# The last quarter of W_down as a plain product, and normed rows in the buffers of W_down's raw quarters

## The chip, the cores and the metric

The kernel runs on one core of one Trainium2 chip, in one launch. The metric is the device time of that launch in microseconds (us), the median over runs. A difference of about 0.2% can be told from no change.

Five engines work side by side: TensorE (PE: matmuls, with PEld for the weight loads), VectorE (DVE), ScalarE (ACT), GpSimd (POOL), and SyncE (SP), which here issues the DMAs. Each takes its instructions strictly in the order fixed when the program was built, and an instruction that waits holds up what stands behind it on its engine.

## What is computed

A two-layer encoder trunk on 512 tokens of width 1024, all in float32. The attention half of a layer is the same in both kernels; the part that matters is the end of each layer:

```python
def reference(x, ...):                       # x: (1, 512, 1024)
    for l in range(2):
        h = rms_norm(x, attn_norm_g[l])
        ...                                  # four mixers and gates give `merged`
        x = x + merged @ w_out[l]            # w_out: 1024 x 1024
        hm = rms_norm(x, mlp_norm_g[l])
        u = jnp.square(jax.nn.relu(hm @ w_up[l]))   # w_up: 1024 x 4096
        x = x + u @ w_down[l]                # w_down: 4096 x 1024
    return x
```

## The kernel before, in words

**Arithmetic.** Each float32 operand is split into a high part `hi` (a cast on ACT, L215) and a low part `lo` (a subtraction on DVE, L216) in the type TensorE reads; `split` does both. A product is three matmuls: hi by hi, hi by lo, lo by hi (`mm3`, L285 to L287, or L1232). The 512 tokens are four tiles of 128 rows (`X[0]` to `X[3]`, tokens t0 to t3), and contraction runs in blocks of 128, eight for 1024 rows.

**Weights.** `chunk` fetches W_in, W_out and W_up in units: a DMA on SP into `w_raw` (three buffers), then a split into `w_hi` and `w_lo` (four buffers each).

**The stages of a layer.** After attention, `run` reads X back (four DMAs, L1274), reads the norm's gain (`norm_g`, L321) and calls `add_rows` for W_out: three chunks of 256, 384 and 384 output columns, four units each, 8 blocks by 4 token tiles by 3 matmuls per chunk (96 matmuls). Each token's sum is added to X on DVE (L1095), and its squares are taken on ACT for the norm. `norm` computes the reciprocal root on DVE, writes normed rows `norm_h` (four buffers of 512 columns, L344), transposes them on TensorE (L222) and splits them into `h_hi` and `h_lo`.

Then come four blocks j of 1024 hidden features. `up(j)` makes the features `u` of block j in eight tiles of 128, with a yield after each. `add_product` multiplies `u` by rows 1024j to 1024j+1023 of W_down with seven products of half-size blocks p0 to p6 (24 matmuls of 512 columns each, 168 in all) in place of the eight that a plain product takes; for that it builds sums of quarters of `u` (`left_sums`: `l_sum`, `l_hi`, `l_lo`) and of W_down (`right_sums`: raw quarters by DMA into `r_raw`, six buffers of 128x1024; sums in place at L1184; `r_hi`, `r_lo`). The product of block j-1 is stepped between the feature tiles of `up(j)`, so its sums are made under matmuls of `up`. The product of the last block, j = 3, has no `up` after it: it runs alone at the end of the layer, and its sums of W_down are made on GpSimd instead of DVE (`alone`, L1219). After that X is written to `x_save` (layer 0, L1296), normed, and the next layer begins; in layer 1 the rows of the result leave by `out_y` (L1212).

**Order.** A scheduler fixes each engine's order when the program is built, from the order of the code, the buffers in each pool and its own estimate of times. An `r_raw` DMA can be put as early as a buffer of its tag is free, so which tiles share buffers has a say in which DMA stands where in SP's queue.

## Time and profile before

| | us |
|---|---|
| median of 3 runs | 1885.83 (1883.5 to 1886.43) |
| the profiled execution, its time | 1886.97 |
| its span, first to last instruction | 1885.2 |
| TensorE busy in it | 1791.2 (95%) |
| VectorE busy | 1310.0 (69%) |
| ScalarE busy | 952.3 (51%) |
| GpSimd busy | 424.5 (23%) |

The page gives shares over the whole span; stages inside it differ, so what follows is read stage by stage, from stretches of the trace. In the trace L216 is one line for every `lo`, and the tile names tell which one it is. A matmul's own duration overlaps its neighbours', so a rate is read from the starts of two matmuls and the count between them. A number in brackets behind a row is the idle time of the engine ahead of it, with what ended that time; `PEclk` is TensorE's granted clock, in tenths by slice or as a share of full speed.

### The profile page before, as it was taken

The numbers are of one execution on the slowest core, as the hardware profiler recorded it, in microseconds if no ns is written. First come the engines' busy times: TensorE is split into PE (matmuls) and PEld (weight loads), VectorE is DVE, ScalarE is ACT, GpSimd is POOL, SyncE is SP. The second block draws the span as 40 slices with busy tenths as digits, with TensorE's granted clock in tenths as the row PEclk, the third lists the DMA queues.
The fourth block names the chain that finished last, engine by engine and source line by source line (L and its number), as shares of the span: only waits on it lengthen the run. The fifth ranks groups of instructions, "written<-read, shape, count | busy, mean of one in ns | idle before, by whom it ended". The sixth has DMA issues, their size and how long they took to land.

```text
span 1885.2 us, 26257 instructions
## 1 busy us (share of the span) xinstructions
PE 1791.2 (95%) x9152; PEld 1538.3 (82%) x9152; DVE 1310.0 (69%) x2623; ACT 952.3 (51%) x1907; POOL 424.5 (23%) x1183
## 2 busy tenths in 40 slices
PE   6998999999999999999799989999999899999997
PEld 5897988787888888888588979887878798888876
DVE  6677866687656367675977878666875655675857
ACT  3565674455433444554446656645553334554543
POOL 2462353323200000000413604632412000000022
PEclk9998999999999999999899989999999999999998
DMA  4312122122244323323132221222222522323221
GB/s 161 119 52 70 57 81 76 51 68 61 88 127 167 101 71 109 115 82 128 56 113 96 75 59 51 78 70 77 64 64 86 196 76 90 116 83 126 81 73 67
DMA packets 64677, 168.70 MB, mean 89 GB/s; under 512 B 7968, under 2 KB 11552, under 8 KB 64544
## 3 DMA queue, kind: packets, MB, share of 16 engines
q1 hardware_dynamic: 64544, 167.02, 28.0%
q8 instruction: 72, 1.18, 0.3%
q14 instruction: 61, 0.50, 0.1%
HBM read 162.80 MB, written 4.19 MB: 89 GB/s over the span
## 4 chain that ended last, share of the span: by engine, by line
PE 74%; DVE 10%; POOL 6%; issue 4%; DMA 3%; ACT 2%; SPq 1%; POOLq 0%; DVEq 0%; ACTq 0%
PE mm L285 17%; PE mm L286 17%; PE mm L287 17%; PE u L1232 10%; PE mm L1232 4%; PE tp L222 4%; PE s L603 2%; DVE w_lo L216 2%; POOL rs_w_qk L235 2%; DMA w_raw<-in_wflat 1%; POOL rs_y_qk L238 1%; POOL rs_w_qk L236 1%; PE y L630 1%; POOL rs_w_qk L237 1%; PE y L629 1%
## 5 line engine op out<-in xcount | busy, mean ns | idle before, releaser
L285 PE MATMUL mm<-h_hi,w_hi 128*128 128x512 f32 (+1 forms) x1104 | 425.4, 387 | 1.8 <-DVE sig L1028 1.0
L287 PE MATMUL mm<-h_hi,w_lo 128*128 128x512 f32 (+1 forms) x1104 | 421.3, 386 | 4.7 <-DVE w_lo L216 2.4
L286 PE MATMUL mm<-h_lo,w_hi 128*128 128x512 f32 (+1 forms) x1104 | 423.8, 385 | 1.4 <-DVE h_lo L216 1.4
L216 DVE TENSOR_TENSOR w_lo<-w_raw,w_hi 128x768 fp32r<-128x768 f32 (+2 forms) x313 | 284.0, 920 | 106.6 <-ACT w_hi L215 104.8
L215 ACT CAST w_hi<-w_raw 128x768 fp32r<-128x768 f32 (+2 forms) x313 | 239.7, 774 | 178.3 <-PE mm L286 92.6
L287 PEld LDWEIGHTS mm<-h_hi,w_lo 128*128 128x128 f32 x1104 | 208.7, 189 | 45.1 <-DVE w_lo L216 3.9
L285 PEld LDWEIGHTS mm<-h_hi,w_hi 128*128 128x128 f32 x1104 | 208.7, 190 | 42.9 <-DVE sig L1028 2.9
L286 PEld LDWEIGHTS mm<-h_lo,w_hi 128*128 128x128 f32 x1104 | 209.1, 190 | 40.4 <-DVE h_lo L216 1.8
L216 DVE TENSOR_TENSOR r_lo<-r_raw,r_hi 128x1024 fp32r<-128x1024 f32 x112 | 145.3, 1298 | 127.1 <-ACT r_hi L215 126.8
L1184 POOL TENSOR_TENSOR r_raw<-r_raw 128x1024 f32<-128x1024 f32 x16 | 47.5, 2974 | 789.7 <-DVE r_lo L216 777.3
L287 PE MATMUL mm<-w_hi,h_lo 128*128 128x384 f32 (+1 forms) x576 | 189.5, 330 | 3.1 <-DVE h_lo L216 3.1
L286 PE MATMUL mm<-w_lo,h_hi 128*128 128x384 f32 (+1 forms) x576 | 189.5, 331 | 1.8 <-DVE w_lo L216 1.7
L285 PE MATMUL mm<-w_hi,h_hi 128*128 128x384 f32 (+1 forms) x576 | 188.8, 333 | 1.0 <-ACT v L529 0.5
L215 ACT CAST r_hi<-r_raw 128x1024 fp32r<-128x1024 f32 x112 | 117.6, 1050 | 110.6 <-PE u L1232 64.6
L235 POOL TENSOR_TENSOR rs_w_qk<-rs_y_qk 128x4 f32<-128x4 f32 (+2 forms) x216 | 62.0, 287 | 364.4 <-DVE rs_y_qk L233 301.4
L1232 PE MATMUL u<-r_lo,l_hi 128*128 128x512 f32 x320 | 128.5, 403 | 8.8 <-DVE r_lo L216 6.3
L1232 PE MATMUL u<-r_hi,l_lo 128*128 128x512 f32 x320 | 128.3, 402 | 5.1 <-DVE l_lo L216 5.1
L1232 PE MATMUL u<-r_hi,l_hi 128*128 128x512 f32 x320 | 123.7, 400 | 6.2 <-ACT l_hi L215 4.7
L287 PEld LDWEIGHTS mm<-w_hi,h_lo 128*128 128x128 f32 x576 | 109.9, 191 | 4.2 <-DVE h_lo L216 3.5
L286 PEld LDWEIGHTS mm<-w_lo,h_hi 128*128 128x128 f32 x576 | 109.9, 191 | 3.6 <-DVE w_lo L216 2.7
L285 PEld LDWEIGHTS mm<-w_hi,h_hi 128*128 128x128 f32 x576 | 109.7, 192 | 2.6 <-ACT v L529 0.7
L1122 ACT ACTIVATE relu<-mm 128x512 f32<-128x512 f32 x64 | 38.3, 599 | 140.0 <-PE mm L287 140.0
(184 smaller groups left out, 3539.4 us busy)
## 6 DMA issues: line engine op xcount, KB each, us to landing
w_raw<-in_wflat SPq DMA_DIRECT2D x232, 384.0 KB, 3.2
r_raw<-in_wflat SPq DMA_DIRECT2D x64, 512.0 KB, 3.5
w_raw<-in_wflat SPq DMA_DIRECT2D x80, 256.0 KB, 2.7
x<-in_x SPq DMA_DIRECT2D x8, 512.0 KB, 6.2
d_full<-in_mask_d SPq DMA_DIRECT2D x8, 448.0 KB, 4.6
x_save<-x SPq DMA_DIRECT2D x4, 512.0 KB, 2.6
x<-x_save SPq DMA_DIRECT2D x4, 512.0 KB, 5.3
out_y<-x SPq DMA_DIRECT2D x8, 256.0 KB, 2.0
```

What stands on the lines that cost most here:

```text
L215: self.nc.scalar.copy(hi, src)
L216: self.nc.vector.tensor_tensor(lo, src, hi.bitcast(F32), op=ALU.subtract)
L222: self.nc.tensor.transpose(out, in_, self.ident_r if short else self.ident)
L235: eng.tensor_tensor(w, y, y, op=ALU.mult)
L236: eng.tensor_tensor(w, w, v, op=ALU.mult)
L285: nc.tensor.matmul(ps, st[0], mv[0], start=first, stop=False)
L286: nc.tensor.matmul(ps, st[0], mv[1], start=False, stop=False)
L287: nc.tensor.matmul(ps, st[1], mv[0], start=False, stop=last)
L603: self.nc.tensor.matmul(ps, q[:, qc], k[:, kc], start=i == 0, stop=i == len(ks) - 1)
L1122: nc.scalar.activation(r, ps, AF.Relu)
L1184: eng.tensor_tensor(a, a, b, op=ALU.add)
L1232: nc.tensor.matmul(ps[q], a[:, k, toks], b, start=first and i == 0, stop=end and i == 2, skip_group_check=True)
```

## The change

The last block (rows 3072 to 4095 of W_down) is no longer an `add_product`. Its `u` is split in four quarters (`left_split`, into a new tag "left" of eight buffers that all left operands share), and `add_rows` multiplies it plainly in chunks of 256, 384 and 384 columns, with W_down's rows through `w_raw`, `w_hi` and `w_lo`: 96 matmuls of 256 columns and 192 of 384, where 168 of 512 stood. The sums on GpSimd and the last block's `l_sum` and `r_*` tiles are gone. While `up(3)` runs, block 2's product is stepped one feature tile later (`j < 3 or i`), so its p6 stands behind `up`'s last feature tile. And `norm` writes its rows as tiles of two halves that, in the two norms inside the MLP part, take buffers of the tag "r_raw".

```diff
@@ -75,7 +75,7 @@
 EVAC = 'act'
 NLO, NHI, NRAW = 4, 4, 3
 
-NLEFT, NRIGHT, NSPLIT = 3, 6, 2
+NLEFT, NRIGHT, NSPLIT = 8, 6, 2
 BACKLOG = 1.0
 STREAM = "D0 gD1 D1 A0 A1 gD2 zD2 gD0 zD0 zD1 B0 B1 B2 gA0 zA0 gA2 C0 zA2 gA1 zA1 C1 gB1 zB1 gC1 gB2 gB0 zB0 zB2 gC0 zC1 zC0 gC2 zC2"
 
@@ -321,7 +321,7 @@
         self.nc.sync.dma_start(g, gain.partition_broadcast(P))
         return g
 
-    def norm(self, pool, X, ms, g):
+    def norm(self, pool, X, ms, g, tag="norm_h", bufs=2):
 
         nc = self.nc
         hi = self.hp.tile([P, KD, S], F32R, name="h_hi", tag="h_hi")
@@ -338,9 +338,10 @@
             for _ in range(3):
                 stt(w, y, y, vh, op0=ALU.mult, op1=ALU.mult)
                 stt(y, w, 1.5, y, op0=ALU.add, op1=ALU.mult)
+            both = pool.tile([P, 2, S], F32, name=tag, tag=tag, bufs=bufs)
             for half in range(2):
                 cs = slice(half * S, half * S + S)
-                h = pool.tile([P, S], F32, name="norm_h", tag="norm_h", bufs=4)
+                h = both[:, half, :]
                 stt(h, X[t][:, cs], y, g[:, cs], op0=ALU.mult, op1=ALU.mult)
                 ps = self.sps.tile([P, 4, P], F32, name="tp", tag="s")
                 for j in range(4):
@@ -1082,15 +1083,15 @@
         return hi, lo
 
 
-    def add_rows(self, pool, X, act, layer, name, k0, ms=None, order=None, out=None):
+    def add_rows(self, pool, X, act, layer, name, k0, ms=None, order=None, out=None, chunks=((0, 256), (256, 384), (640, 384))):
 
         nc = self.nc
-        chunks = list(self.col_chunks(0, D)) if ms is None else [(0, 256), (256, 384), (640, 384)]
         for i, (c0, w) in enumerate(chunks):
             units = self.chunk(layer, name, k0, KD, [(c0, w)], order)
             for t in range(NT):
                 ps = self.mm.tile([P, S], F32, name="mm", tag="mm")
-                self.tm_group(ps[:, 0:w], act, slice(t * P, (t + 1) * P), units)
+                for k, (row, hi, lo) in enumerate(units):
+                    self.mm3(ps[:, 0:w], act(row, t), (hi, lo), k == 0, k == KD - 1)
                 x = X[t][:, c0:c0 + w]
                 nc.vector.tensor_tensor(x, x, ps[:, 0:w], op=ALU.add)
                 if out is not None:
@@ -1130,19 +1131,20 @@
 
 
 
+    def left_split(self, pool, src):
+        hi, lo = (pool.tile([P, KD // 2, S // 2], F32R, name=x, tag="left", bufs=NLEFT) for x in ("l_hi", "l_lo"))
+        self.split(hi, lo, src)
+        return hi, lo
+
     def left_sums(self, pool, x, eng):
 
         h, kh = S // 2, KD // 2
         x11, x12, x21, x22 = x[:, 0:kh, 0:h], x[:, kh:, 0:h], x[:, 0:kh, h:], x[:, kh:, h:]
 
-        def put(src):
-            hi = pool.tile([P, kh, h], F32R, name="l_hi", tag="l_hi", bufs=NLEFT)
-            lo = pool.tile([P, kh, h], F32R, name="l_lo", tag="l_lo", bufs=NLEFT)
-            self.split(hi, lo, src)
-            return hi, lo
+        put = lambda src: self.left_split(pool, src)
 
         def total(a, b, op):
-            s = pool.tile([P, kh, h], F32, name="l_sum", tag="l_sum", bufs=2)
+            s = pool.tile([P, kh, h], F32, name="l_sum", tag="left", bufs=NLEFT)
             eng.tensor_tensor(s, a, b, op=op)
             return s
 
@@ -1199,25 +1201,17 @@
         add(w11, w21)
         yield put(w11)
 
-    def add_product(self, pool, X, x, layer, name, k0, alone, ms=None, out=None):
+    def add_product(self, pool, X, x, layer, name, k0):
 
         nc = self.nc
         n = D // 2
         bank = {}
 
-        def onto(t, nh, ps, op, last=False):
+        def onto(t, nh, ps, op):
             x = X[t][:, nh * n:nh * n + n]
             nc.vector.tensor_tensor(x, x, ps, op=op)
-            if last and out is not None:
-                nc.sync.dma_start(out[t * P:(t + 1) * P, nh * n:nh * n + n], x)
-            if last and ms is not None:
-                part = pool.tile([P, 1], F32, name=f"ms{len(ms[t])}", tag=f"ms{len(ms[t])}", bufs=4)
-                self.squares(pool, x, part)
-                ms[t].append(part)
-
-
-        eng = nc.gpsimd if alone else nc.vector
-        left, right = self.left_sums(pool, x, nc.vector), self.right_sums(pool, layer, name, k0, eng)
+
+        left, right = self.left_sums(pool, x, nc.vector), self.right_sums(pool, layer, name, k0, nc.vector)
         for p, ((hi, lo), w) in enumerate(zip(left, right)):
 
             if p in (0, 1):
@@ -1240,14 +1234,14 @@
                 elif p == 2:
                     onto(q, 1, ps[q], ALU.subtract)
                 elif p == 3:
-                    onto(q, 1, ps[q], ALU.add, True)
+                    onto(q, 1, ps[q], ALU.add)
                 elif p == 4:
                     onto(2 + q, 0, ps[q], ALU.add)
-                    onto(2 + q, 1, ps[q], ALU.subtract, True)
+                    onto(2 + q, 1, ps[q], ALU.subtract)
                 elif p == 5:
-                    onto(q, 0, ps[q], ALU.add, True)
+                    onto(q, 0, ps[q], ALU.add)
                 else:
-                    onto(2 + q, 0, ps[q], ALU.add, True)
+                    onto(2 + q, 0, ps[q], ALU.add)
             yield
 
     def run(self):
@@ -1274,27 +1268,34 @@
                     nc.sync.dma_start(X[t], x_dram[t])
                 g = self.load_gain(pool, I["mlp_norm_g"][layer])
                 ms = [[] for _ in range(NT)]
-                self.add_rows(pool, X, act, layer, "out", 0, ms, self.merges)
-                self.hT = self.norm(pool, X, ms, g)
+                mine = lambda k, t: tuple(x[:, k, t * P:(t + 1) * P] for x in act)
+                self.add_rows(pool, X, mine, layer, "out", 0, ms, self.merges)
+                self.hT = self.norm(pool, X, ms, g, "r_raw", NRIGHT)
                 if not last:
                     g = self.load_gain(pool, I["attn_norm_g"][layer + 1])
                 prev = None
                 for j in range(4):
                     u = pool.tile([P, KD, S], F32, name="u", tag="u", bufs=2)
-                    for _ in self.up(pool, layer, j, u):
-                        if prev is not None:
+                    for i, _ in enumerate(self.up(pool, layer, j, u)):
+
+                        if prev is not None and (j < 3 or i):
                             next(prev, None)
-                    end = j == 3
-                    ms = [[] for _ in range(NT)] if end and not last else None
-                    prev = self.add_product(pool, X, u, layer, "down", j * KD, end, ms, self.out if end and last else None)
-                for _ in prev:
-                    pass
+                    if j < 3:
+                        prev = self.add_product(pool, X, u, layer, "down", j * KD)
+
+                parts = {}
+                for kh in range(2):
+                    for th in range(2):
+                        parts[kh, th] = self.left_split(pool, u[:, 4 * kh:4 * kh + 4, th * (S // 2):(th + 1) * (S // 2)])
+                act = lambda k, t: tuple(x[:, k % 4, t % 2 * P:t % 2 * P + P] for x in parts[k // 4, t // 2])
+                ms = [[] for _ in range(NT)] if not last else None
+                self.add_rows(pool, X, act, layer, "down", 3 * KD, ms, None, self.out if last else None)
                 if not last:
                     xs = self.dram.tile([S, D], F32, name=f"x_save{layer}")
                     x_dram = [xs[t * P:(t + 1) * P, :] for t in range(NT)]
                     for t in range(NT):
                         nc.sync.dma_start(x_dram[t], X[t])
-                    self.hT = self.norm(pool, X, ms, g)
+                    self.hT = self.norm(pool, X, ms, g, "r_raw", NRIGHT)
 
 
 
```

Three places in the engines' orders show what moves. The first is SP's queue from the reads of X at the start of layer 0's MLP part. First the kernel before (`r_raw` here are quarters of W_down for block 0, the first eight `w_raw` the last two chunks of W_out, and the four after them W_up's):

```order
L1274 DMA x_6478<-in_x 128x1024
L1274 DMA x_6479<-in_x 128x1024
L1274 DMA x_6480<-in_x 128x1024
L321 DMA norm_g<-in_mlp_norm_g 128x1024
L1169 DMA r_raw<-in_wflat 128x1024 x6
L248 DMA w_raw<-in_wflat 128x768 x12
L321 DMA norm_g<-in_attn_norm_g 128x1024
```

The changed kernel:

```order
L1268 DMA x_6474<-in_x 128x1024
L1268 DMA x_6475<-in_x 128x1024
L1268 DMA x_6476<-in_x 128x1024
L321 DMA norm_g<-in_mlp_norm_g 128x1024
L248 DMA w_raw<-in_wflat 128x768 x12
L1171 DMA r_raw<-in_wflat 128x1024 x4
L321 DMA norm_g<-in_attn_norm_g 128x1024
L1171 DMA r_raw<-in_wflat 128x1024 x2
```

Twelve `w_raw` now stand ahead of the first `r_raw`, and the six `r_raw` are in two parts around the next norm's gain. Layer 1 shows the same move.

The second place is SP's queue at the end of layer 0. Before, from the last quarters of block 2's W_down to the writes of X:

```order
L1169 DMA r_raw<-in_wflat 128x1024
L248 DMA w_raw<-in_wflat 128x768
L1169 DMA r_raw<-in_wflat 128x1024
L248 DMA w_raw<-in_wflat 128x768 x4
L1169 DMA r_raw<-in_wflat 128x1024 x2
L1296 DMA x_save_9559<-x_6477 128x1024
L1296 DMA x_save_9559<-x_6478 128x1024
L1296 DMA x_save_9559<-x_6479 128x1024
L1296 DMA x_save_9559<-x_6480 128x1024
```

Changed, from block 2's last quarters. Of the five `w_raw` of 128x512 the last four, and of the eleven of 128x768 the first eight, are W_down's last 1024 rows; the seven others of 128x768 are the next layer's first weights:

```order
L1171 DMA r_raw<-in_wflat 128x1024 x2
L248 DMA w_raw<-in_wflat 128x512 x5
L248 DMA w_raw<-in_wflat 128x768 x11
L1297 DMA x_save_9655<-x_6473 128x1024
L1297 DMA x_save_9655<-x_6474 128x1024
L1297 DMA x_save_9655<-x_6475 128x1024
L248 DMA w_raw<-in_wflat 128x768 x3
L1297 DMA x_save_9655<-x_6476 128x1024
L248 DMA w_raw<-in_wflat 128x768
```

The last block's weights now come as `w_raw`; two parts of the next layer's weights stand behind writes of X.

The third is DVE's order at the norm of tokens t2 and t3 between W_out and `up(0)`, layer 0. Before:

```order
L344 SCALAR_TENSOR_TENSOR norm_h<-x_6479,norm_y,norm_g 128x512 x2
L340 SCALAR_TENSOR_TENSOR norm_y<-norm_w,norm_y 128x1
L339 SCALAR_TENSOR_TENSOR norm_w<-norm_y,norm_vh 128x1
L340 SCALAR_TENSOR_TENSOR norm_y<-norm_w,norm_y 128x1
L344 SCALAR_TENSOR_TENSOR norm_h<-x_6480,norm_y,norm_g 128x512 x2
L216 TENSOR_TENSOR h_lo<-tp,h_hi 128x4x128 x4
L216 TENSOR_TENSOR w_lo<-w_raw,w_hi 128x768 x4
L216 TENSOR_TENSOR l_lo<-u,l_hi 128x1024
L216 TENSOR_TENSOR w_lo<-w_raw,w_hi 128x512 x4
L216 TENSOR_TENSOR w_lo<-w_raw,w_hi 128x768 x4
L1146 TENSOR_TENSOR l_sum<-u 128x1024
```

Changed:

```order
L345 SCALAR_TENSOR_TENSOR r_raw<-x_6475,norm_y,norm_g 128x512 x2
L340 SCALAR_TENSOR_TENSOR norm_y<-norm_w,norm_y 128x1
L339 SCALAR_TENSOR_TENSOR norm_w<-norm_y,norm_vh 128x1
L340 SCALAR_TENSOR_TENSOR norm_y<-norm_w,norm_y 128x1
L345 SCALAR_TENSOR_TENSOR r_raw<-x_6476,norm_y,norm_g 128x512 x2
L216 TENSOR_TENSOR h_lo<-tp,h_hi 128x4x128 x2
L216 TENSOR_TENSOR r_lo<-r_raw,r_hi 128x1024
L216 TENSOR_TENSOR h_lo<-tp,h_hi 128x4x128
L216 TENSOR_TENSOR r_lo<-r_raw,r_hi 128x1024
L1186 TENSOR_TENSOR r_raw<-r_raw 128x1024
L216 TENSOR_TENSOR h_lo<-tp,h_hi 128x4x128
L1186 TENSOR_TENSOR r_raw<-r_raw 128x1024
```

Between the `h_lo` of t2 and t3 there now stand the first `r_lo` and a sum of raw quarters of block 0, which before were done during W_out's product.

## Rows read from the trace of the kernel before

**Rows 1.** The page: TensorE's busy time, its clock in 40 slices, one group.
```profile
PE 1791.2 (95%) x9152; PEld 1538.3 (82%) x9152; DVE 1310.0 (69%) x2623; ACT 952.3 (51%) x1907; POOL 424.5 (23%) x1183
...
PEclk9998999999999999999899989999999999999998
```

**Rows 2.** Windows: us; PE, PEld, DVE, ACT, POOL busy (count); PEclk; DMA share; GB/s.
```profile
563.84:603.70 39.86, 36.23 (x194) 35.72 (x193) 25.21 (x53) 14.37 (x30) 0.00 (x0) 0.91 0.47 171
700.00:800.00 100.00, 100.00 (x441) 82.63 (x440) 66.32 (x73) 48.79 (x61) 0.00 (x0) 1.00 0.34 110
899.14:955.11 55.97, 44.43 (x169) 33.50 (x168) 50.86 (x64) 24.25 (x33) 18.75 (x7) 0.88 0.20 66
1492.98:1533.30 40.32, 35.27 (x194) 34.55 (x193) 25.24 (x53) 14.46 (x30) 0.00 (x0) 0.96 0.49 173
1828.76:1881.28 52.52, 44.00 (x169) 33.71 (x167) 42.88 (x37) 19.63 (x20) 17.87 (x7) 0.90 0.14 50
577.00:582.90 5.90, 5.90 (x18) 5.73 (x19) 2.21 (x4) 1.23 (x4) 0.00 (x0) 0.51 0.25 68
```

**Rows 3.** TensorE's timeline, last product of layer 0, two of six waits: start, duration.
```profile
909.46 1.22 PE L1232 MATMUL u<-r_hi,l_hi 128*128 128x512 f32 x2 [4.70 <-ACT l_hi L215]
...
940.20 0.51 PE L1232 MATMUL u<-r_lo,l_hi 128*128 128x512 f32 x1 [2.32 <-DVE norm_v L333]
```

**Rows 4.** DVE and GpSimd there, and a `w_lo` at W_out's end.
```profile
897.04 10.16 DVE L216 TENSOR_TENSOR w_lo<-w_raw,w_hi 128x768 fp32r<-128x768 f32 x4
...
893.62 11.89 POOL L1184 TENSOR_TENSOR r_raw<-r_raw 128x1024 f32<-128x1024 f32 x4 [374.73 <-DVE r_lo L216]
...
602.90 0.96 DVE L216 TENSOR_TENSOR w_lo<-w_raw,w_hi 128x768 fp32r<-128x768 f32 x1
```

**Rows 5.** TensorE's timeline: plain matmuls at full clock, 384 and 256 columns.
```profile
571.13 0.34 PE L285 MATMUL mm<-w_hi,m_hi 128*128 128x384 f32 x1
...
573.04 0.34 PE L287 MATMUL mm<-w_hi,m_lo 128*128 128x384 f32 x1
...
959.00 0.28 PE L286 MATMUL mm<-w_lo,h_hi 128*128 128x256 f32 x1
...
960.91 0.28 PE L287 MATMUL mm<-w_hi,h_lo 128*128 128x256 f32 x1
```

**Rows 6.** W_out's product, layer 0: SP, DVE, ACT and TensorE in turn.
```profile
559.12 5.18 SPq L1169 DMA_DIRECT2D r_raw<-in_wflat  x6
565.31 43.82 SPq L248 DMA_DIRECT2D w_raw<-in_wflat  x12
...
562.76 0.96 DVE L216 TENSOR_TENSOR w_lo<-w_raw,w_hi 128x768 fp32r<-128x768 f32 x1 [0.67 <-ACT w_hi L215]
...
576.12 0.83 ACT L215 CAST w_hi<-w_raw 128x768 fp32r<-128x768 f32 x1 [5.89 <-DMA w_raw<-in_wflat]
...
577.00 1.33 PE L285 MATMUL mm<-w_hi,m_hi 128*128 128x384 f32 x3 [3.62 <-ACT w_hi L215]
```

**Rows 7.** ACT's timeline, W_out's product of layer 1.
```profile
1506.68 0.83 ACT L215 CAST w_hi<-w_raw 128x768 fp32r<-128x768 f32 x1 [6.63 <-DMA w_raw<-in_wflat]
```

**Rows 8.** DVE's last `h_lo` of layer 0's MLP norm; SP's next issues of W_up.
```profile
616.70 1.37 DVE L216 TENSOR_TENSOR h_lo<-tp,h_hi 128x512 fp32r<-128x512 f32 x2 [0.81 <-ACT h_hi L215]
...
625.80 14.53 SPq L248 DMA_DIRECT2D w_raw<-in_wflat  x5
```

**Rows 9.** The page's groups of splits, and its DMA issues with landing times.
```profile
L215 ACT CAST r_hi<-r_raw 128x1024 fp32r<-128x1024 f32 x112 | 117.6, 1050 | 110.6 <-PE u L1232 64.6
...
w_raw<-in_wflat SPq DMA_DIRECT2D x232, 384.0 KB, 3.2
r_raw<-in_wflat SPq DMA_DIRECT2D x64, 512.0 KB, 3.5
```

**Rows 10.** DVE's last sums before the program's end.
```profile
1880.80 1.37 DVE L1210 TENSOR_TENSOR x<-x,mm 128x512 f32<-128x512 f32 x2 [2.40 <-PE mm L1232]
```

**Rows 11.** The page: the load group of one of the plain product's lines.
```profile
L287 PEld LDWEIGHTS mm<-w_hi,h_lo 128*128 128x128 f32 x576 | 109.9, 191 | 4.2 <-DVE h_lo L216 3.5
```

## The prediction, made before the changed kernel ran

> **What bounds the kernel now.** I read the page first, then stretches of the trace where TensorE does not run at its full rate, and last the waits and queues inside those. TensorE is busy 95% of the span, and its clock stands at 8 instead of 9 tenths in four of the forty slices [rows 1]. Each slice is 47.1 us, so the first and the third of them lie in attention, which the change leaves as it is; the other two cover the end of layer 0 and the end of the program. Between 700 and 800 us, in the middle of an MLP part, it is busy for the whole 100 us and starts 441 matmuls, one in 0.2268 us for 512 columns [rows 2]. Nothing off TensorE can gain there. Four stretches differ. The last product of layer 0, 168 matmuls from 899.14 to 955.11 us, takes 55.97 us where 168 x 0.2268 = 38.1 would do; that of layer 1 takes 52.52 [rows 2]. The last two chunks of W_out, 192 matmuls of 384 columns, take 39.86 us in layer 0 and 40.32 in layer 1 [rows 2]; between 571.13 and 573.04 such matmuls start every 1.91/11 = 0.1736 us [rows 5], so 33.3 would do.
>
> In the last product TensorE waits six times for its operands, 4.70 us at the longest and 2.32 near the end [rows 3], and the granted clock averages 0.88 and 0.90 [rows 2]. The operands are late because DVE is: four `w_lo` take 10.16 us, 2.54 each against 0.96 elsewhere, just while GpSimd's four sums of raw quarters run for 11.89 us [rows 4]. In W_out's product TensorE waits 3.62 us for a `w_hi`, whose cast had waited 5.89 us for its `w_raw`. SP issued that one at 565.31, behind six `r_raw` of 512 KB that took 5.18 us to issue, though a raw buffer had been free from 563.72 on, the end of a `w_lo` [rows 6]. Then 18 matmuls take 5.90 us at a granted clock of 0.51, the lower level of 1.2 GHz [rows 2]. In layer 1 the cast waits 6.63 us [rows 7].
>
> **The last block, plain.** It becomes 96 matmuls of 256 columns and 192 of 384. Sixteen steps of 256 columns take 960.91 - 959.00 = 1.91 us, 0.1194 each [rows 5]. So 96 x 0.1194 + 192 x 0.1736 = 11.5 + 33.3 = 44.8 us. Against the measured stretches that is 11.2 us less in layer 0 and 7.7 less in layer 1, 18.9 together, if the plain product runs without waits. What it removes, the sums on GpSimd and six waits, lies inside those stretches and is not counted again.
>
> A rule of the Trainium skill speaks against the narrower pieces: in TensorE: Matmul & The Clock Gate, Back-to-back issue gap, it says that the spacing in a stream of loads and matmuls is set by both, so that narrow matmuls lie above an isolated gap of N/2.4 + 2.5 ns and wide ones below. The rows lie 12 to 14 ns above N/2.4 at 256, 384 and 512 columns alike; by the page's isolated gap the plain product would be an estimated 41.7 us, and the time 6 us lower than below.
>
> Why it should run without waits: the first splits of `u` and of the first four units would be needed as soon as `up(3)`'s last feature tile ends, but p6 of block 2, moved behind that tile, stands between, and it takes 24 x 0.2268 = 5.4 us. In that time the tile's own two passes on ACT and a cast and a subtraction for each of the two late quarters of `u` have to be done, 1.05 us for a cast [rows 9] and about as much for each of the others: 4 to 5 us in a chain. A change of chunk has the shape of W_out's second change of chunk. A unit takes 3.2 us to land [rows 9], 0.83 to cast and 0.96 to subtract [rows 6], 5.0 together, with three raw buffers and 4.2 us of matmuls (24 x 0.1736) per unit of 384 columns. That is close. I take 0.75 us per layer for it, between 0 and 3, the nearest row above being a wait of 2.32 [rows 3]: 1.5 off the gain, 0 to 6.
>
> At the program's end the last sums are one of 384 columns per token instead of two of 512 in 1.37 us [rows 10]; the last then takes about 0.55, a gain of 0.8.
>
> **The queue ahead of W_out.** The normed rows now hold buffers that `r_raw` needs, and in the changed order all twelve `w_raw` stand ahead of the first `r_raw`. The fourth unit of W_out's second chunk can be issued at 563.8, when its buffer comes free, instead of 565.31, and above all has no 3 MB in front of it. It lands some 3.2 us later and is split by 569; the changed order uses it first 46 matmuls into the chunk, near 571.9. So the wait and the low clock after it go: 39.86 - 33.3 = 6.5 us in layer 0 and 7.0 in layer 1, 13.5 together. What is late next is the norm, as before.
>
> **What the sharing adds.** The `r_raw` of block 0 are issued after the twelfth `w_raw`, four of them about when W_out's product ends, two after the normed rows of t2 and t3 have been transposed. W_up's next `w_raw` stand behind them, but those had waited anyway: the twelfth was issued by 609.13 [rows 6], the next at 625.80 [rows 8], so that costs nothing. On ACT two `r_hi` and on DVE two `r_lo` and a sum now stand between the last pieces of `h_hi` and `h_lo`. Before, the last `h_lo` ended at 618.07 [rows 8], just when TensorE took it. Two casts of 1.05 us [rows 9] come ahead of the last `h_hi`, and a sum behind a DMA ahead of the last `h_lo`. Lower bound 0, since `up` has other tokens to work on; upper bound 3, since a late quarter holds DVE for up to its 3.5 us to land [rows 9]. I take 0.7 per layer, nearer to the casts, since the DMA has the whole norm for it: 1.4, 0 to 6.
>
> **The boundary between the layers.** Three `w_raw` of the next layer stand behind the write of t2, which waits for t2's last sum, one group (4.2 us) before the product ends; its 5.0 us to land and be split put it about 1 us past the end, and the write of t3 holds one more. Before, these weights stood ahead of all four writes. The norm of t2 and t3 now also comes at the very end. I take 3 us, between 0 and 6 (the 5.0 of one unit and about 1 of issue).
>
> **The sum.** 18.9 + 13.5 + 0.8 - 1.5 - 1.4 - 3 = 27.3 us. The profiled execution took 1886.97, so 1859.7 in its terms; the median of the runs is 1.1 lower: 1858.6. With no cost at all it would be 1852.7, with all at their upper ends 1870.7.
>
> **Rivals.** First, the earlier weights help less than the order says: the raw buffer comes free only 1.6 us before the old issue, and the reads of X and of the gain, 2.5 MB, are still in flight ahead of it. If half the wait stays in each layer, 6.7 us of the gain goes: 1865.3. Against it, there is slack of 3 us at first use.
>
> Second, the sharing only moves the wait: DVE stands in `up(0)` for a raw quarter, with the `h_lo` of t3 behind it, and TensorE behind that, as long as it stood in W_out's product. Then 13.5 us goes: 1872.1. For it speaks that the last `h_lo` had no slack; against it that the quarters have the time of the norm to land.
>
> Third, weight loads are not hidden under narrow matmuls. A load shows 191 ns [rows 11], longer than the 0.1736 and 0.1194 of a step. If each step took 0.191, the plain product would be 55.0 us, and its 18.9 would turn into -1.5: 1879.0. The Trainium skill has a rule to this end (same page, What overlaps and what doesn't): loads overlap with running matmuls only where the row groups differ, and here all 128 rows are used. The steps in this very kernel speak against it, being shorter than the load they carry.
>
> Fourth, the one that ends slower: the low clock in the plain product. If each unit comes late (5.0 against 4.2 us), TensorE pauses at every unit and is granted the lower level for the rest of the product. At 5.90/18 = 0.328 us per step [rows 2], 192 steps take 63.0 and the product 74.5 us, 18.5 and 22.0 more than before: 27.3 - 18.9 - 40.5 = -32.1, and 1917.9. It decides from the point where 46% of the steps of 384 columns run at that level in both layers (29.7 us lost per layer at 100%, against 27.3 of gain in all). For it: 18 matmuls after one wait of 3.62 us ran so. Against: the last chunk of W_out has the same units and buffers, and no wait.
>
> **How the numbers follow.** The forecast has 0.75, the first rival 0.10, the second 0.08, the third 0.03, the fourth 0.04. The range, 1851 to 1872, takes in the forecast with its unknown costs, the first rival and the edge of the second. A measurement of this kernel can tell about 0.2%, 3.8 us, from no change. Faster by more than that holds for all cases but the fourth and a part of the third: 0.93; within it 0.03; slower 0.04.
>
> **What would show it.** In the profile after, 192 steps of W_out should take 33 to 34 us in both layers, with no wait for `w_hi` over 1 us; the last product some 45 us from p6's end, at a clock near 1.0; GpSimd idle there; `w_lo` near 0.96 each. TensorE waiting for `h_lo` in `up(0)` would speak for the second rival, steps over 0.18 us at full clock for the third, a clock near 0.5 in the last product for the fourth. The prediction is wrong if the boundary between the layers, about which the trace of before says least, costs more than 10 us.

## The result: 1855.1 us, 1.6% less

The changed kernel takes 1855.12 us (median of four runs, 1854.15 to 1855.92) against 1884.96 for the kernel before beside it: a ratio of 0.9841, 95% interval 0.9824 to 0.9859. The forecast was 1858.6, with a range from 1851 to 1872. The profiled execution took 1855.32 us, its span 1853.5, which is 31.7 us less than the span before.

The page of the changed kernel, its parts 1 and 2 (busy time and share of each engine; granted clock in 40 slices), answers to [rows 1]:

```profile
PE 1788.4 (96%) x9392; PEld 1556.9 (84%) x9392; DVE 1253.4 (68%) x2601; ACT 937.1 (51%) x1905; POOL 378.2 (20%) x1167
...
PEclk9998999999999999999999999999999999999999
```

TensorE runs 240 matmuls more in about the same busy time, and of the four dips of the clock one is left, in attention. The two at the ends of the layers are gone; those in attention come and go, since a second profile of the changed kernel has its one dip in layer 1's attention (slice 24) and none in layer 0's. The windows of the same four stretches as in [rows 2] (us; busy time of PE, PEld, DVE, ACT, POOL with counts; clock; DMA share; GB/s): W_out's last two chunks and the last product, layer 0, then both in layer 1:

```profile
564.80:598.09 33.29, 33.29 (x194) 33.27 (x193) 18.11 (x47) 12.38 (x28) 0.00 (x0) 1.00 0.34 111
893.51:938.82 45.31, 45.31 (x289) 45.27 (x288) 22.45 (x55) 15.86 (x34) 0.00 (x0) 1.00 0.31 105
1475.86:1509.14 33.28, 33.28 (x194) 33.27 (x193) 18.09 (x47) 12.26 (x28) 0.00 (x0) 1.00 0.35 115
1804.57:1849.88 45.31, 45.31 (x289) 45.14 (x287) 15.01 (x22) 7.52 (x9) 0.00 (x0) 1.00 0.26 86
```

In each of them TensorE is busy for the whole stretch at full clock; DVE, which was busy for 50.86 of 55.97 us in the last product of layer 0, has 22.45 of 45.31 left. The span is made of these pieces:

| piece | before, us | after, us | gained | forecast |
|---|---|---|---|---|
| up to W_out's second chunk, layer 0 | 563.85 | 564.81 | -1.0 | 0 |
| its 192 matmuls, both layers | 39.86 + 40.32 | 33.29 + 33.28 | 13.6 | 13.5 |
| from there to the last product, both layers | 295.44 + 295.46 | 295.42 + 295.43 | 0.0 | -1.4 |
| last product, both layers | 55.97 + 52.52 | 45.31 + 45.31 | 17.9 | 17.4 |
| end of layer 0 to W_out's second chunk, layer 1 | 537.87 | 537.04 | 0.8 | -3.0 |
| last matmul to the end | 3.92 | 3.62 | 0.3 | 0.8 |

What TensorE has to do up to W_out's second chunk is the same in all kernels below, and yet that chunk begins at 561.6 to 564.8 us in their profiles. The stretch between the layers varies too: 537.0 us here, 537.7 in the second profile of the same kernel, and 536.0 to 540.5 in all the kernels below but one. A difference of 3 us between two profiles therefore means little unless the stretch that it lies in is known, and the 0.8 us in the table is not to be told from nothing.

The weights of W_out come early now. SP, ACT and TensorE's waits (us in total, times, longest) in the changed kernel, to be held against [rows 6]:

```profile
564.70 38.82 SPq L248 DMA_DIRECT2D w_raw<-in_wflat  x12
603.57 2.02 SPq L1171 DMA_DIRECT2D r_raw<-in_wflat  x4
...
568.82 0.83 ACT L215 CAST w_hi<-w_raw 128x768 fp32r<-128x768 f32 x1 [0.64 <-DMA w_raw<-in_wflat]
```

```profile
PE mm L285 <- DVE x L1096: 1.4, 1, 1.4
PE mm L286 <- DVE h_lo L216: 0.7, 1, 0.7
PE mm L285 <- ACT h_hi L215: 0.3, 1, 0.3
```

The cast that had waited 5.89 us waits 0.64, and from 560 to 700 us TensorE waits for no weight. DVE's timeline in the norm shows the queue that the prediction feared, and [rows 8] is its counterpart:

```profile
610.53 1.23 DVE L216 TENSOR_TENSOR r_lo<-r_raw,r_hi 128x1024 fp32r<-128x1024 f32 x1 [0.26 <-ACT r_hi L215]
611.67 0.68 DVE L216 TENSOR_TENSOR h_lo<-tp,h_hi 128x512 fp32r<-128x512 f32 x1
612.27 1.22 DVE L216 TENSOR_TENSOR r_lo<-r_raw,r_hi 128x1024 fp32r<-128x1024 f32 x1
613.41 1.22 DVE L1186 TENSOR_TENSOR r_raw<-r_raw 128x1024 f32<-128x1024 f32 x1
614.54 0.69 DVE L216 TENSOR_TENSOR h_lo<-tp,h_hi 128x512 fp32r<-128x512 f32 x1
```

The last `h_lo` ends 17.1 us after W_out's last matmul (615.23 - 598.10), where it was 14.4 before, and nobody waits for it; the wait of 0.7 us for an `h_lo` above is there in the other kernels too. The `h_lo` ahead of the last one is waited for. It stands behind the first `r_lo`, and ends at 612.35:

```profile
611.77 0.52 PE L285 MATMUL mm<-h_hi,w_hi 128*128 128x256 f32 x3
612.41 0.39 PE L286 MATMUL mm<-h_lo,w_hi 128*128 128x256 f32 x1
```

Three steps take 0.64 us where they take 0.36 elsewhere [rows 5]. This is what the queue costs, 0.3 to 0.4 us per layer: from W_out's end to the last product takes 295.42 us in the changed kernel and 295.09 in the one below that differs from it only in the rows' buffers. Against the kernel before (295.44) nothing is lost, because the plain product saves as much in the same stretch.

### The profile page after: what moved, and what is told of

Its sections match the earlier page's. It is cut to its first block, busy times and chain, and to the rows that moved or that the text cites. A ratio compares the mean times of both kernels' runs of the same rounds, so it can differ in the third digit from the quotient of the medians.

```text
span 1853.5 us, 26743 instructions
## 1 busy us (share of the span) xinstructions
PE 1788.4 (96%) x9392; PEld 1556.9 (84%) x9392; DVE 1253.4 (68%) x2601; ACT 937.1 (51%) x1905; POOL 378.2 (20%) x1167
## 4 chain that ended last, share of the span: by engine, by line
PE 80%; DVE 7%; POOL 5%; issue 3%; ACT 2%; DMA 2%; SPq 0%; POOLq 0%; DVEq 0%; ACTq 0%
PE mm L285 20%; PE mm L286 20%; PE mm L287 19%; PE u L1226 9%; PE tp L222 4%; PE mm L1226 4%; PE s L604 2%; POOL rs_w_qk L235 1%; PE y L631 1%; PE y L630 1%; DVE w_lo L216 1%; POOL rs_y_qk L238 1%; POOL rs_w_qk L236 1%; POOL rs_w_qk L237 1%; DMA x<-in_x 1%
## 5 line engine op out<-in xcount | busy, mean ns | idle before, releaser
L216 DVE TENSOR_TENSOR w_lo<-w_raw,w_hi 128x768 fp32r<-128x768 f32 (+2 forms) x337 | 299.6, 899 | 125.7 <-ACT w_hi L215 123.5
L215 ACT CAST w_hi<-w_raw 128x768 fp32r<-128x768 f32 (+2 forms) x337 | 258.4, 774 | 220.2 <-PE mm L286 105.5
L216 DVE TENSOR_TENSOR r_lo<-r_raw,r_hi 128x1024 fp32r<-128x1024 f32 x84 | 102.7, 1222 | 93.2 <-ACT r_hi L215 93.2
L215 ACT CAST r_hi<-r_raw 128x1024 fp32r<-128x1024 f32 x84 | 88.4, 1052 | 74.2 <-PE u L1226 47.7
L216 DVE TENSOR_TENSOR pt_lo<-tp,pt_hi 128x256 fp32r<-128x256 f32 (+2 forms) x144 | 77.8, 551 | 37.5 <-ACT pt_hi L215 30.3
L215 ACT CAST pt_hi<-tp 128x256 fp32r<-128x256 f32 (+2 forms) x144 | 66.8, 479 | 63.0 <-PE tp L222 50.8
L1226 PE MATMUL u<-r_hi,l_lo 128*128 128x512 f32 x240 | 93.6, 390 | 0.0
L1226 PE MATMUL u<-r_lo,l_hi 128*128 128x512 f32 x240 | 93.4, 389 | 0.0
```

The lines of the kernel that those rows point to most:

```text
L215: self.nc.scalar.copy(hi, src)
L216: self.nc.vector.tensor_tensor(lo, src, hi.bitcast(F32), op=ALU.subtract)
L1226: nc.tensor.matmul(ps[q], a[:, k, toks], b, start=first and i == 0, stop=end and i == 2, skip_group_check=True)
```

## Experiments

The ratio is to the kernel before, run beside each; W_out is the 192 matmuls of its last two chunks, "last" the product of block 3 alone, each from its first matmul's start to one step past its last one's, in layers 0 and 1, from the profile.

| kernel | median, us | ratio (95%) | W_out, us | last, us |
|---|---|---|---|---|
| before | 1884.96 | 1 | 39.9, 40.3 | 56.0, 52.5 |
| changed | 1855.12 | 0.9841 (0.9824 to 0.9859) | 33.3, 33.3 | 45.3, 45.3 |
| changed, again | 1856.01 | 0.9841 (0.9827 to 0.9854) | 33.3, 33.3 | 45.3, 45.3 |
| plain product, own rows | 1864.50 | 0.9890 (0.9876 to 0.9905) | 39.5, 39.2 | 45.3, 45.3 |
| shared buffers alone | 1870.75 | 0.9927 (0.9910 to 0.9943) | 33.3, 33.3 | 54.6, 51.2 |
| before, quarters held back | 1873.76 | 0.9941 (0.9928 to 0.9955) | 33.3, 33.3 | 54.6, 51.1 |
| before, quarters on GpSimd's queue | 1884.45 | 1.0000 (0.9990 to 1.0010) | 40.9, 42.4 | 52.3, 49.3 |
| before, sums on DVE | 1870.71 | 0.9928 (0.9914 to 0.9943) | 39.6, 39.7 | 50.4, 45.3 |
| shared, sums on DVE | 1865.39 | 0.9895 (0.9872 to 0.9917) | 33.3, 33.3 | 50.4, 51.0 |
| the same, later step, three split buffers | 1859.53 | 0.9867 (0.9846 to 0.9888) | 33.3, 33.3 | 44.2, 46.3 |
| changed, step as before | 1854.47 | 0.9839 (0.9824 to 0.9853) | 33.3, 33.3 | 45.6, 45.3 |
| changed, loads doubled | 1856.89 | 0.9855 (0.9834 to 0.9877) | 33.3, 33.3 | 45.3, 45.3 |
| changed, narrow chunk last | 1854.23 | 0.9833 (0.9820 to 0.9846) | 33.3, 33.3 | 45.1, 45.1 |

### Either part alone

The plain product with the normed rows in buffers of their own:

```diff
-                self.hT = self.norm(pool, X, ms, g, "r_raw", NRIGHT)
+                self.hT = self.norm(pool, X, ms, g)
...
-                    self.hT = self.norm(pool, X, ms, g, "r_raw", NRIGHT)
+                    self.hT = self.norm(pool, X, ms, g)
```

> The changed kernel with one part undone: the normed rows have buffers of their own again, the last block stays plain. In this kernel's order the six r_raw stand ahead of W_out's twelve w_raw again. Theory (the shared buffers alone bring W_out's weights forward): the 192 matmuls of W_out's last two chunks take 39 to 41 us again in both layers with a cast that waits 5 to 7 us for its w_raw, the last products stay at 45 us, and the time is 1855.1 + 13.6 = 1868.7 (1866 to 1871). Rival (the earlier weights come from the plain product, or from the plan as a whole): 1855 to 1858, and no wait in W_out's product.

And the other way round, the kernel before with the change's `norm` and its two calls, and nothing else of it:

> The kernel before with the other part alone: normed rows in the buffers of the raw quarters, the last block still by block sums on GpSimd. Theory: W_out's 192 matmuls take 33.3 us in both layers, the last products 56 and 52.5 as before, nothing new in up(0), so 1885.0 - 13.6 = 1871.4 (1869 to 1874). Rival (the wait moves into up(0), where h_lo stands behind r_lo, and the plain product hid that): 1878 to 1885, with waits of 2 us or more on h_lo in up(0).

The first came out at 1864.5, the second at 1870.75. TensorE's waits in the first, between 540 and 640 us and between 1440 and 1560:

```profile
PE mm L285 <- ACT w_hi L215: 3.4, 1, 3.4
PE mm L285 <- DVE x L1096: 1.6, 1, 1.6
...
PE mm L285 <- ACT w_hi L215: 4.2, 1, 4.2
PE mm L285 <- DVE x L1096: 1.0, 1, 1.0
```

The wait for the weights is back with the buffers, and W_out is 12.1 us longer in sum, as the theory has it. The whole time rises by 9.4 only, 4.2 less than forecast. Of that, by the profiles, 1.5 us lie in W_out (12.1 instead of 13.6), 0.7 are what the sharing had cost behind W_out, and 2.0 come from a second chunk that begins earlier than in the changed kernel's first profile, in the part of the program that the edit does not touch. The second run fits its forecast (14.4 us gained for 13.6), though not in every piece: the last products are 2.7 us shorter in sum where they were expected unchanged, and from W_out's end to the last product it takes 0.4 us more per layer than before, with no wait of the 2 us that the rival needs. The gains of the two runs add up to 35.1 us, those of the changed kernel to 29.8; the 2.7 and the 1.5 us are part of that, since they lie in the stretch that the other part shortens. So the parts overlap a little, and the shared buffers alone bring W_out's weights forward.

### Why the quarters hurt: their place in SP's queue, their bytes, or the sums made of them

```diff
-                nc.sync.dma_start(raw, self.ins["wflat"][off:off + P * kk * n].rearrange("(p k n) -> p k n", p=P, k=kk))
+                nc.gpsimd.dma_start(raw, self.ins["wflat"][off:off + P * kk * n].rearrange("(p k n) -> p k n", p=P, k=kk))
                 got.append(raw)
```

> The kernel before with one edit: the DMAs of W_down's raw quarters are issued by GpSimd instead of SP, everywhere. In SP's order W_out's twelve w_raw then follow the gain directly, but the six r_raw still go out at the same time and use the same DMA engines. It tells whether W_out's weights were late because they stood behind the r_raw in SP's order, or because 3 MB were on the way at that moment. Theory A (order): the cast waits at most 2 us, W_out's 192 matmuls take 33 to 35 us. Theory B (bytes on the way): the cast waits 4 to 6.5 us as before and they take 38 to 40 us. The whole time is less telling, since GpSimd also makes the last block's sums: 1870 to 1890.

No time was gained (1884.45), and W_out was slower than before, so SP's order as such is not it. But the second theory does not fit either, since its weight came 4 us earlier and another engine was late. In its timeline GpSimd issues the quarters, SP the weights; ACT casts the late unit; DVE is the one to watch:

```profile
557.32 3.37 POOL L1169 DMA_DIRECT2D r_raw<-in_wflat  x6 [38.53 <-DVE m_lo L1080]
...
563.56 46.42 SPq L248 DMA_DIRECT2D w_raw<-in_wflat  x12
...
572.08 0.84 ACT L215 CAST w_hi<-w_raw 128x768 fp32r<-128x768 f32 x1 [2.69 <-DMA w_raw<-in_wflat]
...
573.99 1.23 DVE L1184 TENSOR_TENSOR r_raw<-r_raw 128x1024 f32<-128x1024 f32 x1 [2.21 <-DMA r_raw<-in_wflat]
576.07 1.23 DVE L1184 TENSOR_TENSOR r_raw<-r_raw 128x1024 f32<-128x1024 f32 x1 [0.86 <-DMA r_raw<-in_wflat]
577.56 1.22 DVE L1184 TENSOR_TENSOR r_raw<-r_raw 128x1024 f32<-128x1024 f32 x1 [0.26 <-DMA r_raw<-in_wflat]
578.70 0.95 DVE L216 TENSOR_TENSOR w_lo<-w_raw,w_hi 128x768 fp32r<-128x768 f32 x1
...
579.71 0.69 PE L286 MATMUL mm<-w_lo,m_hi 128*128 128x384 f32 x1 [5.95 <-DVE w_lo L216]
```

The cast is done at 572.9, but the subtraction of the same unit stands behind four sums of block 0's quarters in DVE's order, and these wait for their own DMAs until 577.56. TensorE waits 5.95 us, for DVE this time. (The last products are 6.9 us shorter in sum than in the kernel before, which this run was not made to explain; the whole time stays the same.) The kernel before had the same queue on DVE, hidden by the later DMA:

```profile
574.00 2.37 DVE L1184 TENSOR_TENSOR r_raw<-r_raw 128x1024 f32<-128x1024 f32 x2 [0.24 <-DMA r_raw<-in_wflat]
576.98 0.96 DVE L216 TENSOR_TENSOR w_lo<-w_raw,w_hi 128x768 fp32r<-128x768 f32 x1 [0.61 <-ACT w_hi L215]
```

DVE was through with the sums at 576.37, about when ACT got its weight (576.12). Two waits of about the same length stood side by side. In the run with GpSimd's queue the quarters also landed later, so that the sums ended at 578.78; but with the sums as they were before, the subtraction could have begun at 576.37 instead of 576.98, 0.6 us earlier, however early its weight came. Taking the DMA's wait away alone gains next to nothing. The shared buffers move both, since quarters that come late have late sums. That was then tried without sharing: a one-element write from the last normed row into each quarter's tile holds its DMA back.

```diff
                 raw = pool.tile([P, kk, n], F32, name="r_raw", tag="r_raw", bufs=NRIGHT)
+                if k0 == 0:
+                    nc.vector.tensor_copy(raw[:, 0, 0:1], self.hT[1][:, KD - 1, S - 1:S].bitcast(F32))
```

> The kernel before, no buffers shared and block sums kept; the DMAs of block 0's raw quarters are held back by a one-element write into each r_raw tile from the last normed row (eight small DVE instructions per layer), so that they and the sums made of them come after W_out's product. It tells whether it is the lateness of these quarters and of their sums that helps, or something else in the shared buffers. Theory (lateness of the quarters with their work on ACT and DVE): W_out's 192 matmuls take 33.3 us in both layers and the time is 1870 to 1874, as with the shared buffers alone (1870.75). Rival (the sharing did it in another way): 1880 to 1887.

W_out takes 33.29 us in both layers, the time is 1873.76. It is 3.0 us above the shared buffers alone, with intervals that overlap, and 2.0 of that is in view: from W_out's end to the last product it takes 296.14 and 297.52 us, against 295.85 and 295.86, with waits of 0.3 and 1.5 us for a `w_lo` in `up(0)`. So it is the lateness of the quarters that helps, by whatever means; the shared buffers are one way to get it. No run here holds back the sums alone: that both the DMAs and the sums had to move is read from the two waits above.

### What was slow in the block sums

```diff
-        eng = nc.gpsimd if alone else nc.vector
+        eng = nc.vector
```

> The kernel before, with the last block's sums of raw quarters made on DVE like those of the other blocks, not on GpSimd. It tells why the block sums were slow when they ran alone. Theory A (DVE has too much to do in that product, whoever makes the sums): w_lo falls back to 0.96 us each, but DVE gets eight sums of some 1.2 us per layer, and the products still take 50 to 56 us: 1875 to 1888. Theory B (GpSimd's sums slowed DVE, and that alone made the product slow): the products fall to about 45 us or less, 1866 or lower.

It gained 14.5 us, below the span of theory A and short of theory B. The `w_lo` that had taken 2.54 us each on DVE [rows 4] take 0.91:

```profile
896.81 1.82 DVE L216 TENSOR_TENSOR w_lo<-w_raw,w_hi 128x768 fp32r<-128x768 f32 x2
```

and the windows of the two last products (columns as above) are

```profile
897.96:948.37 50.41, 42.93 (x170) 31.77 (x169) 46.68 (x69) 24.10 (x33) 0.00 (x0) 0.97 0.21 73
1819.57:1864.64 45.07, 40.42 (x168) 30.70 (x167) 40.24 (x43) 19.55 (x20) 0.00 (x0) 1.00 0.17 59
```

The second window ends with the start of the last matmul, 0.2 us short of the table's end. DVE's busy time in these products falls from 50.86 to 46.68 us and from 42.88 to 40.24 though it has the sums to make as well, and over the whole span from 1310.0 to 1306.7 with 16 instructions more: GpSimd cost DVE more than it took off it. The Trainium skill (SBUF — State Buffer, SBUF: two separate sides) says that DVE and GpSimd share a port pair, and that of a DVE instruction with two inputs in SBUF and a GpSimd instruction that reads SBUF, the one that starts first holds the pair for its whole length and the other is blocked. The trace agrees in that a `w_lo` took 2.54 us beside GpSimd's sums and 0.91 without them; it does not show who held the pair. Both theories had a part: GpSimd was in the way, and with it gone DVE is busy for 46.68 of 50.41 us in layer 0, where it also has the norm and the next weights.

That raises the question whether the plain product was needed. Two kernels, the shared buffers with the sums on DVE, and the same with block 2's product stepped later and a third buffer each for `r_hi` and `r_lo`:

```diff
-NLEFT, NRIGHT, NSPLIT = 3, 6, 2
+NLEFT, NRIGHT, NSPLIT = 3, 6, 3
...
-                    for _ in self.up(pool, layer, j, u):
-                        if prev is not None:
+                    for i, _ in enumerate(self.up(pool, layer, j, u)):
+                        if prev is not None and (j < 3 or i >= 1):
                             next(prev, None)
+                    for _ in prev or ():
+                        pass
```

> Normed rows in the buffers of the raw quarters, and the last block still by block sums, all of them on DVE (both earlier runs' edits in one kernel). Theory: the two gains lie in different places and add: 1885.2 - 14.4 - 14.5 = 1856.3 (1854 to 1859), level with the changed kernel, so that the plain product as such is worth nothing against block sums made on DVE. Rival: DVE's earlier work in up(0) pushes its sums back, and part of the gain is lost: 1860 to 1868.

> As e9_share_dve, with two edits more: block 2's product is stepped one feature tile later in up(3), so that its p6 covers the first splits of the last block, and r_hi and r_lo have three buffers each instead of two (room that the shared buffers freed). Theory A (the waits that remain in the last product are at its start and at each change of product, for a buffer of r_hi): the last products fall by 2 to 6 us in each layer, 1847 to 1853, below both kernels. Theory B (DVE is the bound there: it is busy 46.7 of 50.4 us and 40.2 of 45.1 us): 1853 to 1857, no gain worth the name.

They came out at 1865.4, in the rival's range, and at 1859.5, above both theories. In the first the gains did not add: of the 9 us that are missing, 5.7 are in layer 1's last product, 50.81 us instead of 45.07. Its window (to the start of its last matmul, as above), and TensorE's timeline at its longest wait:

```profile
1808.68:1859.49 50.81, 43.34 (x168) 32.58 (x167) 40.44 (x43) 19.53 (x20) 0.00 (x0) 0.93 0.15 52
```

```profile
1837.19 0.79 PE L1233 MATMUL u<-r_lo,l_hi 128*128 128x512 f32 x1 [2.72 <-DVE r_lo L216]
1837.79 0.63 PE L1233 MATMUL u<-r_hi,l_lo 128*128 128x512 f32 x1
1838.21 0.63 PE L1233 MATMUL u<-r_lo,l_hi 128*128 128x512 f32 x1
1838.64 0.63 PE L1233 MATMUL u<-r_hi,l_lo 128*128 128x512 f32 x1
```

After a wait of 2.72 us the matmuls start every 0.43 us, the lower clock; in the kernel before with the sums on DVE, the longest wait of that product was 1.23 and the clock stayed at 1.00. Why that `r_lo` came later here was not followed. The rival's number was right and its reason was not: `up(0)` has no wait above the 0.7 us of the other kernels.

In the second kernel the last products fall by 6.2 and 4.8 us, as theory A had it, but the time falls by 5.9 only. p6 and the last product together take 49.7 and 51.7 us, against 50.7 in both layers of the changed kernel. In layer 0 DVE is busy for 48.75 of the 49.67: it is the bound there, and the cover and the buffers do not change that. In layer 1 it is not so busy (43.6 us), but a wait of 2.67 us for an `r_hi` is followed by the lower clock. What is lost lies between the layers: 542.3 us, 1.8 more than in any other profile here and 5.2 more than in the changed kernel's, of which 1.9 are waits at the start; the rest is not settled. Block sums with fewer matmuls come level with the plain product in the last stretch and do not beat it; in layer 0 because DVE has to make what they save on TensorE.

### How safe the plain product is

The first of the next two undoes the later step; the second loads each unit of the last block twice.

```diff
-                        if prev is not None and (j < 3 or i):
+                        if prev is not None:
```

> The changed kernel with block 2's product stepped as before, so that its p6 ends ahead of up(3)'s last feature tile and the plain product follows that tile at once. Theory A (p6 behind the tile is needed as cover, as the prediction had it): a wait of about 3.5 us (two passes on ACT of 0.6, a cast of 1.05, a subtraction of 1.2) at the start of the plain product in both layers, then some us at the lower clock: 1862 to 1875. Theory B (the first 48 matmuls use the two quarters of u that are ready earlier and cover it): 1855 to 1858, no wait above 1 us.

```diff
-        nc.sync.dma_start(raw, self.ins["wflat"][off:off + P * kk * n].rearrange("(p k n) -> p k n", p=P, k=kk))
+        [nc.sync.dma_start(raw, self.ins["wflat"][off:off + P * kk * n].rearrange("(p k n) -> p k n", p=P, k=kk)) for _ in range(2 if name == "down" else 1)]
```

> The changed kernel with each weight unit of the last block loaded twice into the same buffer, the second load after the first, so that a unit takes about 2 x 3.2 + 0.83 + 0.96 = 8.2 us from issue to split instead of 5.0. It measures how far the plain product was from the prediction's slow rival (units late, TensorE at the lower clock). Theory A (three raw buffers give room: a unit is wanted every 4.2 us and 8.2/3 = 2.7 us is what three buffers need): at most 3 us per layer, 1855 to 1861. Theory B (the chain at a change of chunk has no room): 5 us or more of waits per layer, the lower clock after them, 1870 or more.

The early step costs nothing (1854.47): TensorE goes from `up` to the plain product without a gap,

```profile
890.90 0.40 PE L287 MATMUL mm<-h_hi,w_lo 128*128 128x512 f32 x1
891.13 0.41 PE L285 MATMUL mm<-w_hi,l_hi 128*128 128x256 f32 x2
```

and the product takes 45.62 and 45.32 us. The first matmuls use the quarters of `u` that were ready before. The doubled loads do not show at all in the windows of the product,

```profile
891.93:937.24 45.31, 45.31 (x289) 45.27 (x288) 20.04 (x54) 16.06 (x34) 0.00 (x0) 1.00 0.53 176
1806.03:1851.34 45.31, 45.31 (x289) 45.14 (x287) 15.07 (x22) 7.52 (x9) 0.00 (x0) 1.00 0.51 156
```

though the DMA engines' share rises from 0.31 to 0.53. So the estimated 8.2 us of a unit, spread over three buffers, were early enough, and the lower clock did not come. Just behind the product, in the next layer's first chunk, TensorE does wait 1.8 us for an `h_lo`, which the changed kernel does not.

Last, the order of the chunks:

```diff
-                self.add_rows(pool, X, act, layer, "down", 3 * KD, ms, None, self.out if last else None)
+                self.add_rows(pool, X, act, layer, "down", 3 * KD, ms, None, self.out if last else None, ((0, 384), (384, 384), (768, 256)))
```

> The changed kernel with the last block's chunks in the order 384, 384, 256 columns instead of 256, 384, 384. The last sums and writes of the program are then a third smaller. Theory A: only the end moves, by 0.3 to 0.6 us: 1854 to 1856, not to be told from the changed kernel. Theory B (the first units, now wider, are split too late for the first matmuls, or the last change of chunk, with shorter groups ahead of it, has no room): waits of 1 us or more in the product, 1857 to 1865.

> The changed kernel as it is, on the same chip as the two others, to compare them with: 1854 to 1856.5, and the end of attention within 1 us of its place in the first profile.

1854.23 (1851.38 to 1856.71) and 1856.01 (1853.35 to 1856.57) overlap. The second profile of the changed kernel missed one of its expectations: W_out's second chunk, right behind attention, begins 1.5 us earlier than in the first, where 1 us was expected at most. Nothing here beats the changed kernel by more than it can be measured.

## The prediction, step by step

**The bound and the four stretches** were right: 31.5 of the 31.7 us of span came from them.

**The plain product** was forecast at 44.8 us and took 45.3, with the loads hidden behind the steps as the rows had it. By the isolated gap of the Trainium skill (TensorE: Matmul & The Clock Gate, Back-to-back issue gap), which the prediction weighed, it would have taken an estimated 41.7 us; the measurement stays with the rows. The 0.75 us per layer for the changes of chunk were nearly the 0.5 that it took, but not for that reason: TensorE waited for nothing there. What it had too small was the step: 384 columns took 0.176 us with these operands (1848.13 to 1849.71 in nine steps of layer 1's product) instead of 0.1736.

**The queue ahead of W_out** gave 13.6 us for 13.5, but its reason was half of it. The step that failed is "above all has no 3 MB in front of it" as the whole cause: with the weights ahead in SP's queue and the quarters still loaded early, nothing was gained (1884.45 us). DVE's sums of those quarters were as late, in the same order on DVE as `w_lo`, and the rows of DVE in that stretch, which the prediction did not use, showed it. The forecast came out because the changed order moves the sums as well; in this the prediction was lucky.

**The operands are late because DVE is**: right, and GpSimd's part in it is now measured, 14.5 us of the whole time by one edit.

**The cover by p6** was wrong as a need: without it the time is the same.

**The costs** were mis-sized. The sharing's 1.4 us were 0.7: TensorE waits 0.3 to 0.4 us per layer, for the `h_lo` ahead of the last one, not for the last, which came 2.8 us later without anyone waiting for it. So the rival's "no slack" for the last `h_lo` was a misreading. The plain product saves the 0.7 again in the same stretch. Of the boundary's 3 us nothing is to be seen: SP does issue three weights after the write of t2, the first at 937.88, 0.95 us before TensorE begins on the next layer at 938.83, but the subtraction for it ends at 943.85, in time for the order on TensorE, which waits for no weight there.

```profile
930.63 5.18 SPq L1297 DMA_DIRECT2D x_save<-x  x3
937.88 2.38 SPq L248 DMA_DIRECT2D w_raw<-in_wflat  x3
940.41 0.34 SPq L1297 DMA_DIRECT2D x_save<-x  x1
943.87 0.33 SPq L248 DMA_DIRECT2D w_raw<-in_wflat  x1
```

TensorE's only wait between 935 and 960 us is 0.2 us for an `h_hi`, as before. In spans the gain is 31.7 us for 27.3 forecast: 1.4 and 3.8 more from these two stretches and 0.6 from the four pieces above, less 1.0 by which attention happened to be longer in this profile and 0.5 at the program's end (0.3 for 0.8). In medians the forecast is 3.5 us too high; the rest is that the profiled execution lay 1.1 us above its median before, and 0.2 after.

**The rivals.** The first (half of the wait stays) did not come, and of the second (the wait moves into `up(0)`) only the 0.3 to 0.4 us above; the experiment with GpSimd's queue shows that a wait does move, to DVE, when only SP's order is changed. The third, unhidden loads, is excluded by 289 matmuls in 45.31 us, 0.157 each with loads of 0.187 to 0.190. The fourth did not come, and not with doubled loads either.

## What to carry to other kernels

When an engine waits for a transfer, look on every engine of that stretch for what would be late next: here a wait of about the same length stood on DVE behind the same early transfers, so reordering the DMAs alone gained nothing, and holding back the early work as a whole gained all of it. Loading ahead is only free if the work that it sets off fits ahead too. An algorithm with fewer matmuls pays only while the engine that prepares its operands has time; at the end of a layer, with nothing to hide the preparation under, 288 plain matmuls were as fast as the 168 with sums at their best (with p6, 101.5 us in both layers against 101.4).

## What the runs showed of the hardware

GpSimd's sums made DVE's subtractions beside them take 2.54 us instead of 0.91 to 0.96. A wait of 2.72 us was followed by steps of 0.43 us for 512 columns instead of 0.2268, a granted clock at the lower level, while 1.23 us was not. The length of one wait does not decide it: in layer 1's last product a wait of 2.33 us for an `r_lo` was followed by the lower clock (0.50 from 1866.36 us) in the kernel before, and by the full clock (1.00 from 1854.72 us) in the one with the quarters held back. Steps at full clock of 256 and 384 columns (0.12 and 0.176 us) stayed shorter than the load of 0.187 to 0.191 us that each carries.
